# A depthwise convolution of 31 taps, wholly as multiply-adds on VectorE

## The chip, the cores and the metric

The kernel runs on one core of one Trainium2 chip. The metric is the device time of one execution in microseconds (us). A core has five engines that run side by side, each in its own order: TensorE (PE; its weight loads are shown as PEld), VectorE (DVE), ScalarE (ACT), GpSimd (POOL) and SyncE (SP), which issues DMAs.

## The reference

A two-layer hybrid backbone over 256 latent and 256 context tokens, width 1024. Layer 0 runs attention (8 heads, 2 key/value heads) beside a convolution module of 512 channels; both share one input projection `w_in` and one output projection `w_o`. A SwiGLU follows, then a Mamba-2 layer and a mixture of 8 experts. The change lies in `conformer_conv`:

```python
def depthwise_conv(x, w, b):
    width = w.shape[0]                                   # 31
    y = lax.conv_general_dilated(x, w[:, None, :].astype(x.dtype), window_strides=(1,),
                                 padding=[(width // 2, width // 2)],
                                 dimension_numbers=('NWC', 'WIO', 'NWC'),
                                 feature_group_count=x.shape[-1])
    return y + b

def conformer_conv(u, dw_w, dw_b, ln_g, ln_b):
    a, g = jnp.split(u, 2, axis=-1)
    h = depthwise_conv(a * jax.nn.sigmoid(g), dw_w, dw_b)
    return jax.nn.silu(layer_norm(h, ln_g, ln_b))

def even_mixer(...):
    ...
    a_lat = latent_attention(q, k, v, kc, vc)
    b_lat = conformer_conv(u, dw_w, dw_b, ln_g, ln_b)
    y = jnp.concatenate([a_lat, b_lat], axis=-1) @ w_o
    ...
```

The context tokens go through the same functions with the same weights.

## The kernel before

Tokens lie along the free dimension (512: two streams `s` of 256), channels on the 128 partitions, so the convolution's 512 channels are four chunks of 128x512. A product in full precision is three matmuls (`mm3`, lines 243 to 245): each factor is split into a high part that TensorE reads exactly and a rest. For weights ScalarE casts the high part (L161) and VectorE subtracts (L164), 128x1024 at a time; for activations the same is done by L133 and L134.

`even_u` computes the two halves of the projection; at its end VectorE multiplies them into `pad` (L527), four chunks with 15 zeros on each side of a stream, and starts the generator `even_conv` in the background. `even_conv` takes the chunks in two pairs. Tap 0 is ScalarE's (L545). Taps 1 to 17 are multiply-adds on VectorE, `scalar_tensor_tensor` (L568): `acc = pad[shifted] * weight + acc`, one for each tap and chunk, 68 in all, 128x512 each. Taps 18 to 30 (`NPE = 13`) are products on TensorE: for each tap and chunk ScalarE multiplies the identity by the tap's weights into a diagonal matrix (`dg`, L559), GpSimd makes the diagonal of their rest (L560), and `mm3` accumulates into one PSUM bank (`c<-t,dg`): 52 taps, 156 matmuls. For these `pad` is split once a chunk (L133, L134), and at the end VectorE adds the bank to `acc` (L573), four times. The tap weights are split in `columns2` (L314, L315).

`even_ln` follows on the same generator, across the 512 channels, which are partitions: products with a matrix of ones sum the four chunks (L583, c = 0 to 3) to the mean (L585); the chunks are centred (L589), squared (L591) and summed again (L593); VectorE reduces (L597), GpSimd makes the factor (L428, L430), TensorE broadcasts it (L602). Then each chunk is multiplied (L607), goes through silu on ScalarE (L609), and is split (L133, L134) into the factors k = 4 to 7 of the output projection; k = 0 to 3 come from attention.

What is written first: `phase1` goes through a list of units (the key/value and q projections, the groups of adaLN matmuls, L347, whose weights come by DMA), and after each piece of weights `tick` lets each background generator run to its next `yield` (the convolution once, an attention generator twice). So the convolution's taps, the attention (q and k norms L635 to L661, scores L752, transposes of probabilities L784, products with V L775) and the projections are interleaved. After the list, `drain` finishes the generators, and the units of `w_o` follow (`g<-whl,t` in the trace). A scheduler then fixes each engine's order from dependences and its own clock; on the chip each engine runs its list strictly in that order.

Of the kernel before, what the change touches and what calls it, by code (L numbers as in the profile page):

```python
# [10 lines left out]
F32 = mybir.dt.float32  # L11
F32R = mybir.dt.float32r
# [3 lines left out]
ALU = mybir.AluOpType  # L16
# [3 lines left out]
P = 128  # L20
# [70 lines left out]
class Net:  # L91
# [210 lines left out]
    def columns2(self):  # L302
        A, cols, row = self.A, self.cols_fn, self.row_fn
        kc = self.ecp.tile([P, NCONST - C_LE], F32, name="kc")
        self.nc.sync.dma_start(kc, A["kc"][:, C_LE:NCONST])
        self.LE, self.GE, self.GT = (kc[:, c - C_LE:c - C_LE + P] for c in (C_LE, C_GE, C_GT))
        self.cosd, self.sind = (kc[:, c - C_LE:c - C_LE + P].rearrange("p (b d) -> p b d", b=2) for c in (C_COS, C_SIN))
        c2 = cols("c2", [row(A["ev_norm2"][0]), row(A["ev_dw_b"][0]), row(A["ev_ln_g"][0]), row(A["ev_ln_b"][0])], self.wp)
        self.n2e, self.dwb, self.lng, self.lnb = c2[:, 0:8], c2[:, 8:12], c2[:, 12:16], c2[:, 16:20]
        w = cols("dww", [A["ev_dw_w"][0].rearrange("t (c p) -> (t c) p", p=P)], self.wp)  # L310
        self.dww = w.rearrange("p (t c) -> p t c", c=4)
        wh = self.wp.tile([P, 124], F32R, name="dwh")
        wl = self.wp.tile([P, 124], F32, name="dwl")
        self.nc.scalar.copy(wh, w)  # L314
        self.nc.vector.tensor_sub(wl, w, wh.bitcast(F32))  # L315
        self.dwl = wl.rearrange("p (t c) -> p t c", c=4)

    def columns3(self):
        A, cols, row = self.A, self.cols_fn, self.row_fn
# [74 lines left out]
    def row(self, col):  # L394

        nc = self.nc
        pt = self.ps()
        nc.tensor.transpose(pt[:8, 0:P], col, self.ident)
        r = self.wk([8, P], "row", bufs=1)
        nc.scalar.copy(r, pt[:8, 0:P])  # L400
        d = self.drp.tile([8, P], F32, name=self.nm("drow"))
        nc.sync.dma_start(d, r)
        return d
# [86 lines left out]
    R_NORM = 1  # L490


    NPE = 13

    def even_u(self, h):

# [40 lines left out]
    def even_conv(self):  # L537

        nc = self.nc
        nd = 31 - self.NPE  # L540
        for c0 in (0, 2):
            acc, hl = [], []
            for c in (c0, c0 + 1):
                a = self.cacc[:, c].rearrange("p (s t) -> p s t", s=2)
                nc.scalar.activation(a, self.pad[:, c, :, 0:256], AF.Identity, scale=self.dww[:, 0, c:c + 1],  # L545
                                     bias=self.dwb[:, c:c + 1])
                acc.append(a)
                x = self.wk([P, 2, 2, 286], "t8", F32R)
                self.split(x[:, 0], x[:, 1], self.pad[:, c])
                hl.append(x)  # L550
            pe = [(j, t) for j in range(2) for t in range(nd, 31)]
            n = max(nd - 1, self.NPE)
            done = None
            for i in range(n):
                for j, t in pe[2 * i:2 * i + 2]:
                    if t == nd:
                        pc = self.ps("c")
                    d = [self.wk([P, P], f"dg{q}", F32R, bufs=4) for q in range(2)]
                    nc.scalar.mul(d[0], self.ident, self.dww[:, t, c0 + j:c0 + j + 1])  # L559
                    nc.gpsimd.tensor_scalar(d[1], self.ident, self.dwl[:, t, c0 + j:c0 + j + 1], None,  # L560
                                            op0=ALU.mult)
                    self.mm3(pc.rearrange("p (s t) -> p s t", s=2), d,
                             (hl[j][:, 0, :, t:t + 256], hl[j][:, 1, :, t:t + 256]), t == nd, t == 30)
                    if t == 30:
                        done = j, pc
                if i + 1 < nd:
                    for j in range(2):
                        nc.vector.scalar_tensor_tensor(acc[j], self.pad[:, c0 + j, :, i + 1:i + 257],  # L568
                                                       self.dww[:, i + 1, c0 + j:c0 + j + 1], acc[j],
                                                       op0=ALU.mult, op1=ALU.add)  # L570
                if done:
                    j, q = done
                    nc.vector.tensor_tensor(acc[j], acc[j], q.rearrange("p (s t) -> p s t", s=2), op=ALU.add)  # L573
                    done = None
                yield
        yield from self.even_ln()

# [1297 lines left out]
```

## Time and profile before

| | before |
|---|---|
| median of 3 runs | 1913.47 us (1911.69 to 1915.6) |
| profiled execution | 1911.85 us, span 1910.1 us, mean granted TensorE clock 0.961 |
| TensorE busy | 1778.9 us, 93% of the span (weight loads 58%) |
| VectorE busy | 703.5 us, 37% |
| ScalarE busy | 519.1 us, 27% |
| GpSimd busy | 174.1 us, 9% |

The span begins with the profiled execution's first instruction; rows give microseconds from there. Shares over the span mix stages with different limits: the expert stage, most of the span, is TensorE and DMA with VectorE almost idle, and the convolution lies between 88 and 200 us. TensorE takes a matmul of two 32-bit factors as two records, so a count in a row can be twice the program's. The record of an instruction may overlap the next one's: where the text speaks of spacing it is the time from one start to the next.

### The profile page before, as it was taken

How to read it: one execution, taken by the hardware profiler on the slowest of the kernel's cores; microseconds unless marked ns; L12 is line 12 of the kernel's file. 1: busy time of each engine (PE TensorE's matmuls, PEld its weight loads, DVE VectorE, ACT ScalarE, POOL GpSimd, SP SyncE). 2: the span in 40 equal slices, each digit the busy share in tenths (PEclk: the TensorE clock that was granted, in tenths of full speed). 3: DMA queues.
4: the chain of work that ended last, by engine and by line, in shares of the span. 5: the costliest groups of instructions: out<-in, count | busy, mean ns of one | idle time of the engine just before them, and what ended most of it. 6: DMA issues, size and time to landing. Idle time of an engine off the chain costs nothing. (4 is left out here: it accounts for less than half of the span.)

```text
span 1910.1 us, 33591 instructions
## 1 busy us (share of the span) xinstructions
PE 1778.9 (93%) x14384; PEld 1110.9 (58%) x14384; DVE 703.5 (37%) x1143; ACT 519.1 (27%) x969; POOL 174.1 (9%) x167
## 2 busy tenths in 40 slices
PE   6999998999999989989989999999999999899964
PEld 3675356788888868757667445445644463435411
DVE  3395546334334356798887110101110101002001
ACT  3434454231222335756874100100000000001000
POOL 0064000000000014133320000000000000000000
PEclk8999999999999999989899899999999999999976
DMA  8543765422323243323357899999999999999995
GB/s 319 178 157 120 250 184 189 135 96 89 109 89 98 81 142 103 122 84 115 101 197 279 320 399 418 416 418 416 418 416 417 417 417 412 414 419 413 417 413 230
DMA packets 131574, 497.87 MB, mean 261 GB/s; under 512 B 11312, under 2 KB 18392, under 8 KB 102744
## 3 DMA queue, kind: packets, MB, share of 16 engines
q1 hardware_dynamic: 126808, 487.25, 66.3%
q10 hardware_dynamic: 4608, 8.39, 1.3%
q8 instruction: 115, 1.88, 0.4%
q14 instruction: 43, 0.35, 0.1%
HBM read 494.45 MB, written 1.15 MB: 259 GB/s over the span
## 5 line engine op out<-in xcount | busy, mean ns | idle before, releaser
L1533 PE MATMUL h<-raw,xe 128*32 128x512 f32 (+1 forms) x2664 | 265.6, 551 | 15.8 <-DMA raw<-in_od_ex_w_dram 15.8
L244 PE MATMUL g<-t,whl 128*128 128x512 f32 (+1 forms) x608 | 237.4, 390 | 0.0
L243 PE MATMUL g<-t,whl 128*128 128x512 f32 (+1 forms) x608 | 234.8, 396 | 2.1 <-ACT opad L1057 1.9
L245 PE MATMUL g<-t,whl 128*128 128x512 f32 (+1 forms) x608 | 232.7, 390 | 0.8 <-POOL whl L164 0.8
L1533 PE MATMUL h<-t,xe 128*32 128x384 f32 (+1 forms) x2200 | 214.9, 543 | 7.7 <-DMA t<-in_od_ex_w_dram 7.7
L164 DVE TENSOR_TENSOR whl<-raw,whl 128x1024 fp32r<-128x1024 f32 x109 | 137.7, 1266 | 206.6 <-ACT whl L161 206.1
L161 ACT CAST whl<-raw 128x1024 fp32r<-128x1024 f32 x129 | 134.5, 1049 | 269.9 <-PE g L245 234.3
L1533 PEld LDWEIGHTS h<-raw,xe 128*32 128x32 f32 x2664 | 97.8, 111 | 175.2 <-issue 113.2
L1544 DVE TENSOR_TENSOR g<-g,h 128x512 f32<-128x512 f32 (+1 forms) x38 | 23.6, 621 | 425.9 <-PE h L1533 238.6
L244 PE MATMUL g<-whl,t 128*128 128x512 f32 (+1 forms) x432 | 168.0, 392 | 9.2 <-DVE whl L164 7.3
L245 PE MATMUL g<-whl,t 128*128 128x512 f32 (+1 forms) x432 | 164.4, 389 | 0.0
L243 PE MATMUL g<-whl,t 128*128 128x512 f32 (+1 forms) x432 | 160.5, 394 | 1.9 <-DVE t L641 1.8
L1533 PEld LDWEIGHTS h<-t,xe 128*32 128x32 f32 x2200 | 79.1, 110 | 136.1 <-issue 91.8
L1598 PE MATMUL y<-raw,hT 128*32 128x256 f32 x2512 | 144.7, 388 | 9.7 <-DMA raw<-in_od_ex_w_dram 9.7
L1541 ACT ACTIVATE g<-h 128x512 f32<-128x512 f32 (+1 forms) x38 | 20.7, 544 | 448.9 <-PE h L1533 448.9
L243 PEld LDWEIGHTS g<-t,whl 128*128 128x128 f32 x608 | 116.6, 192 | 29.3 <-ACT opad L1057 2.3
L244 PEld LDWEIGHTS g<-t,whl 128*128 128x128 f32 x608 | 116.3, 191 | 23.7 <-issue 1.0
L245 PEld LDWEIGHTS g<-t,whl 128*128 128x128 f32 x608 | 115.4, 190 | 24.2 <-POOL whl L164 1.0
L428 POOL TENSOR_SCALAR rsv<-sst 128x1 f32<-128x1 f32 (+1 forms) x15 | 4.7, 311 | 1295.0 <-DVE sst L421 1294.8
L1598 PEld LDWEIGHTS y<-raw,hT 128*32 128x32 f32 x2512 | 80.0, 112 | 72.4 <-DMA raw<-in_od_ex_w_dram 15.0
L1598 PE MATMUL y<-t,hT 128*32 128x256 f32 x1744 | 103.4, 395 | 10.7 <-DMA t<-in_od_ex_w_dram 10.7
L1612 DVE TENSOR_TENSOR ys<-y,g2r 128x512 f32<-128x512 f32 (+1 forms) x12 | 6.6, 577 | 260.6 <-PE y L1598 260.6
(349 smaller groups left out, 2091.1 us busy)
## 6 DMA issues: line engine op xcount, KB each, us to landing
raw<-in_od_ex_w_dram SPq DMA_DIRECT2D x138, 1024.0 KB, 18.0
t<-in_od_ex_w_dram SPq DMA_DIRECT2D x102, 1024.0 KB, 19.2
raw<-in_od_ex_w_dram SPq DMA_DIRECT2D x68, 768.0 KB, 15.0
t<-in_od_ex_w_dram SPq DMA_DIRECT2D x60, 768.0 KB, 15.8
raw<-in_ev_ff_w_dram SPq DMA_DIRECT2D x32, 1024.0 KB, 5.1
raw<-in_ev_ada_w_dram SPq DMA_DIRECT2D x24, 1024.0 KB, 6.7
raw<-in_od_ada_w_dram SPq DMA_DIRECT2D x24, 1024.0 KB, 5.2
raw<-in_od_w_in_dram SPq DMA_DIRECT2D x20, 1024.0 KB, 5.2
```

Source lines behind the costliest of these rows:

```text
L161: self.nc.scalar.copy(hv, v[:, k0:k0 + m])
L164: eng.tensor_tensor(lv, v[:, k0:k0 + m], hv.bitcast(F32), op=ALU.subtract)
L243: mm(out, l[0], r[0], start=start, stop=False)
L244: mm(out, l[0], r[1], start=False, stop=False)
L245: mm(out, l[1], r[0], start=False, stop=stop)
L428: nc.gpsimd.tensor_scalar(v[:, :m], ss, inv_n, EPS, op0=ALU.mult, op1=ALU.add)
L1533: nc.tensor.matmul(st[i][g][32 * p:32 * p + 32, :n], st["x"][:, k, 32 * g:32 * g + 32], wv[:, n * p:n * p + n], start=k == 0, stop=k == KD ...
L1541: nc.scalar.activation(st["g"][g], st[0][g][:, :n], AF.Silu)
L1544: nc.vector.tensor_mul(st["g"][g], st["g"][g], st[1][g][:, :n])
L1598: nc.tensor.matmul(st["y"][g // 2][32 * q:32 * q + 32, g % 2 * 256:g % 2 * 256 + 256], st["hT", s][:, c, g, 32 * p:32 * p + 32], wv[:, 256 ...
L1612: nc.vector.tensor_tensor(ys[:, g:g + m], st["y"][g // 2][:, :256 * m].rearrange("p (g n) -> p g n", g=m), self.g2.unsqueeze(1).to_broadca ...
```

## The change

`even_conv` computes all of the taps 1 to 30 as multiply-adds on VectorE, 120 where there were 68. Each turn (from one `yield` to the next) holds one tap of both chunks of a pair, so a pair has 30 turns where it had 17. The diagonals, their 156 matmuls, the split of `pad`, the four additions from PSUM and the split of the tap weights are gone. `even_ln` and all else are as before; lines behind the change carry lower numbers (L568 is L543 now, L583 is L554, L602 is L573, L347 is L342, L752 is L723, L784 is L755, L660 is L631, L661 is L632, L637 is L608, L641 is L612, L653 is L624, L687 and L707 and others fall likewise).

```diff
--- before.py
+++ after.py
@@ -309,11 +309,6 @@
         self.n2e, self.dwb, self.lng, self.lnb = c2[:, 0:8], c2[:, 8:12], c2[:, 12:16], c2[:, 16:20]
         w = cols("dww", [A["ev_dw_w"][0].rearrange("t (c p) -> (t c) p", p=P)], self.wp)
         self.dww = w.rearrange("p (t c) -> p t c", c=4)
-        wh = self.wp.tile([P, 124], F32R, name="dwh")
-        wl = self.wp.tile([P, 124], F32, name="dwl")
-        self.nc.scalar.copy(wh, w)
-        self.nc.vector.tensor_sub(wl, w, wh.bitcast(F32))
-        self.dwl = wl.rearrange("p (t c) -> p t c", c=4)
 
     def columns3(self):
         A, cols, row = self.A, self.cols_fn, self.row_fn
@@ -490,7 +485,6 @@
     R_NORM = 1
 
 
-    NPE = 13
 
     def even_u(self, h):
 
@@ -537,41 +531,18 @@
     def even_conv(self):
 
         nc = self.nc
-        nd = 31 - self.NPE
         for c0 in (0, 2):
-            acc, hl = [], []
+            acc = []
             for c in (c0, c0 + 1):
                 a = self.cacc[:, c].rearrange("p (s t) -> p s t", s=2)
                 nc.scalar.activation(a, self.pad[:, c, :, 0:256], AF.Identity, scale=self.dww[:, 0, c:c + 1],
                                      bias=self.dwb[:, c:c + 1])
                 acc.append(a)
-                x = self.wk([P, 2, 2, 286], "t8", F32R)
-                self.split(x[:, 0], x[:, 1], self.pad[:, c])
-                hl.append(x)
-            pe = [(j, t) for j in range(2) for t in range(nd, 31)]
-            n = max(nd - 1, self.NPE)
-            done = None
-            for i in range(n):
-                for j, t in pe[2 * i:2 * i + 2]:
-                    if t == nd:
-                        pc = self.ps("c")
-                    d = [self.wk([P, P], f"dg{q}", F32R, bufs=4) for q in range(2)]
-                    nc.scalar.mul(d[0], self.ident, self.dww[:, t, c0 + j:c0 + j + 1])
-                    nc.gpsimd.tensor_scalar(d[1], self.ident, self.dwl[:, t, c0 + j:c0 + j + 1], None,
-                                            op0=ALU.mult)
-                    self.mm3(pc.rearrange("p (s t) -> p s t", s=2), d,
-                             (hl[j][:, 0, :, t:t + 256], hl[j][:, 1, :, t:t + 256]), t == nd, t == 30)
-                    if t == 30:
-                        done = j, pc
-                if i + 1 < nd:
-                    for j in range(2):
-                        nc.vector.scalar_tensor_tensor(acc[j], self.pad[:, c0 + j, :, i + 1:i + 257],
-                                                       self.dww[:, i + 1, c0 + j:c0 + j + 1], acc[j],
-                                                       op0=ALU.mult, op1=ALU.add)
-                if done:
-                    j, q = done
-                    nc.vector.tensor_tensor(acc[j], acc[j], q.rearrange("p (s t) -> p s t", s=2), op=ALU.add)
-                    done = None
+            for t in range(1, 31):
+                for j in range(2):
+                    nc.vector.scalar_tensor_tensor(acc[j], self.pad[:, c0 + j, :, t:t + 256],
+                                                   self.dww[:, t, c0 + j:c0 + j + 1], acc[j],
+                                                   op0=ALU.mult, op1=ALU.add)
                 yield
         yield from self.even_ln()
 
```

VectorE, around the split of the last q weights (`L164 whl`), in the second pair of chunks; `t_55` is the convolution's accumulator, `kn`, `gs`, `gc` and `ss` belong to the norm and rotation of k and q. Before:

```order
L568 SCALAR_TENSOR_TENSOR t_55_261<-pad_262,dww,t_55_261 128x512
L661 TENSOR_TENSOR kn_1107<-t_209_1116,t_210_1118 128x128
L568 SCALAR_TENSOR_TENSOR t_55_261<-pad_262,dww,t_55_261 128x512
L659 TENSOR_TENSOR t_219_1166<-t_218_1164,gs_477 128x64 x2
L568 SCALAR_TENSOR_TENSOR t_55_261<-pad_262,dww,t_55_261 128x512
L660 TENSOR_TENSOR t_218_1164<-t_218_1164,gc_476 128x128
L164 TENSOR_TENSOR whl_995<-raw_913,whl_995 128x1024
L661 TENSOR_TENSOR kn_1155<-t_218_1164,t_219_1166 128x128
L637 TENSOR_REDUCE ss_1204<-t_222_1202 128x8
L641 TENSOR_TENSOR t_226_1210<-g_1000,rs_1208 128x512
```

And with the change:

```order
L543 SCALAR_TENSOR_TENSOR t_55_261<-pad_262,dww,t_55_261 128x512 x4
L631 TENSOR_TENSOR t_162_968<-t_162_968,gc_472 128x128
L164 TENSOR_TENSOR whl_828<-raw_760,whl_828 128x1024
L543 SCALAR_TENSOR_TENSOR t_55_261<-pad_262,dww,t_55_261 128x512 x4
L632 TENSOR_TENSOR kn_959<-t_162_968,t_163_970 128x128
L543 SCALAR_TENSOR_TENSOR t_55_261<-pad_262,dww,t_55_261 128x512 x4
L608 TENSOR_REDUCE ss_1008<-t_166_1006 128x8
L543 SCALAR_TENSOR_TENSOR t_55_261<-pad_262,dww,t_55_261 128x512 x6
L612 TENSOR_TENSOR t_170_1014<-g_833,rs_1012 128x512
L543 SCALAR_TENSOR_TENSOR t_55_261<-pad_262,dww,t_55_261 128x512 x4
L624 TENSOR_TENSOR t_134_832<-t_170_1014,qkg_469 128x2x4x64
```

Single multiply-adds stood between two steps of the norms; now there are up to six. The split stands behind 69 of the 120 multiply-adds; in the program before it was behind 54 of 68.

TensorE, around the products with ones that sum the chunks (`c<-t_55,ones`), between the attention's scores (`g<-kT,t`), transposes (`t<-ka,pe`) and an adaLN group (`g<-raw,cs`). Before:

```order
L784 MATMUL t_1515<-ka,pe_1380 128x128
L784 MATMUL t_1515<-ka,pe_1397 128x128
L784 MATMUL t_1515<-ka,pe_1437 128x128
L583 MATMUL c_2119<-t_55_261,ones 128x512 x3
L784 MATMUL t_1508<-ka,pe_1454 128x128
L784 MATMUL t_1515<-ka,pe_1454 128x128
L347 MATMUL g_1578<-raw_1410,cs 32x512 x4
L347 MATMUL g_1578<-raw_1467,cs 32x512 x4
L752 MATMUL g_1599<-kT_841,t_181_998 128x256
```

And with the change:

```order
L723 MATMUL g_1161<-kT_702,t_133_831 128x256
L723 MATMUL g_1186<-kT_702,t_133_831 128x256
L554 MATMUL c_1850<-t_55_261,ones 128x512
L723 MATMUL g_1187<-kT_702,t_133_831 128x256
L723 MATMUL g_1203<-kT_702,t_133_831 128x256
L678 MATMUL t_1093<-ka,t_134_832 128x128 x4
L723 MATMUL g_1204<-kT_702,t_133_831 128x256
L554 MATMUL c_1850<-t_55_261,ones 128x512 x3
L342 MATMUL g_1222<-raw_1099,cs 32x512 x4
```

The products of chunks 1 to 3 stand earlier among the attention's work, ahead of the transposes of probabilities. Between them and the first product of `w_o` TensorE's list now holds 8 scores of 256 columns where it held 4, 72 adaLN matmuls where it held 64, 96 transposes of probabilities where it held 90, 4 transposes of q where it held none; the product of chunk 3, which stood there alone, is gone from there.

TensorE, behind the broadcast of the layer norm's factor (`c<-ka,rs`); `t_272` before and `t_205` with the change are the high part of k = 4 of the output projection, the first chunk behind silu, and `t_271`, `t_273`, `t_204`, `t_206` are factors that come from attention. Before:

```order
L243 MATMUL g_2287<-whl_2256,t_271_1372 128x512
L244 MATMUL g_2287<-whl_2256,t_271_1372 128x512
L602 MATMUL c_2222<-ka,rs_2199 128x128 x4
L245 MATMUL g_2287<-whl_2256,t_273_1374 128x512
L243 MATMUL g_2285<-whl_2259,t_271_1372 128x512
...
L245 MATMUL g_2288<-whl_2259,t_273_1374 128x512
L398 MATMUL t_2418<-ka,ac_114 8x128
L243 MATMUL g_2285<-whl_2264,t_272_1373 128x512
```

And with the change:

```order
L244 MATMUL g_1952<-whl_1923,t_204_1139 128x512
L245 MATMUL g_1952<-whl_1923,t_206_1141 128x512
L393 MATMUL t_2082<-ka,ac_114 8x128
L393 MATMUL t_2089<-ka,ac_114 8x128
L573 MATMUL c_1892<-ka,rs_1890 128x128 x4
L342 MATMUL c_2257<-raw_2127,cs 32x512 x4
L342 MATMUL c_2257<-raw_2129,cs 32x512 x4
L243 MATMUL g_1949<-whl_1928,t_205_1140 128x512
L244 MATMUL g_1949<-whl_1928,t_205_1140 128x512
```

Thirty products of the output projection that need no silu stood between the broadcast and the first that does; now an adaLN group of 8 matmuls (`c<-raw,cs`) stands there alone, and those products are ahead of the broadcast. That group stood in the stage behind `w_o` before.

## Rows read from the trace of the kernel before

**Rows 1.** Busy time in two stretches (us; in brackets the instructions); granted clock; DMA share
```profile
core 0: us, PE busy (x) PEld busy (x) DVE busy (x) ACT busy (x) POOL busy (x), PEclk, DMA share, GB/s
89.00:198.00 109.00, 103.81 (x535) 70.92 (x533) 87.51 (x164) 46.19 (x112) 55.38 (x64) 0.97 0.42 147
198.00:270.00 72.00, 68.15 (x334) 26.36 (x330) 34.71 (x84) 32.35 (x76) 0.00 (x0) 1.00 0.68 213
```

**Rows 2.** Costliest groups: shapes, count | busy us, mean ns | idle ahead, what ended it
```profile
L568 DVE SCALAR_TENSOR_TENSOR t<-pad,dww,t 128x512 f32<-128x512 f32 x68 | 49.6, 765 | 0.0
L243 PE MATMUL c<-t,dg 128*128 128x512 f32 x52 | 21.5, 414 | 1.1 <-DVE t L573 1.1
L560 POOL TENSOR_SCALAR dg<-ka,dwl 128x128 fp32r<-128x128 f32 x52 | 44.3, 865 | 104.8 <-DVE dwl L315 53.9 <-PE c L245 50.5
```

**Rows 3.** TensorE in order of time: start, duration us, line, tiles, count
```profile
98.53 0.39 PE L243 MATMUL c<-t,dg 128*128 128x512 f32 x1
...
100.63 0.40 PE L243 MATMUL c<-t,dg 128*128 128x512 f32 x1
```

**Rows 4.** ScalarE in order of time, one cast of the key and value weights
```profile
102.40 2.00 ACT L161 CAST whl<-raw 128x1024 fp32r<-128x1024 f32 x2 [0.64 <-DMA raw<-in_ev_w_in_dram]
```

**Rows 5.** VectorE in order of time, first half of the convolution
```profile
88.86 2.06 DVE L527 TENSOR_TENSOR pad<-t,t 128x512 f32<-128x512 f32 x3 [11.24 <-ACT t L526]
...
97.37 7.64 DVE L568 SCALAR_TENSOR_TENSOR t<-pad,dww,t 128x512 f32<-128x512 f32 x10
104.93 0.68 DVE L355 TENSOR_TENSOR ar<-ar,t 128x512 f32<-128x512 f32 x1
105.53 1.21 DVE L164 TENSOR_TENSOR whl<-raw,whl 128x1024 fp32r<-128x1024 f32 x1
...
111.84 2.72 DVE L568 SCALAR_TENSOR_TENSOR t<-pad,dww,t 128x512 f32<-128x512 f32 x4
114.49 0.67 DVE L573 TENSOR_TENSOR t<-t,c 128x512 f32<-128x512 f32 x1
...
119.54 0.27 DVE L637 TENSOR_REDUCE ss<-t 128x2 f32<-128x128 f32 x1
```

**Rows 6.** VectorE in order of time, a wait and the last multiply-add
```profile
150.27 0.69 DVE L637 TENSOR_REDUCE ss<-t 128x8 f32<-128x512 f32 x1 [3.76 <-ACT t L635]
...
197.03 0.75 DVE L568 SCALAR_TENSOR_TENSOR t<-pad,dww,t 128x512 f32<-128x512 f32 x1
197.69 0.61 DVE L764 TENSOR_SCALAR pe<-pe,rc 128x256 f32<-128x256 f32 x2
```

**Rows 7.** TensorE in order of time, around the matmuls with ones
```profile
191.81 1.13 PE L752 MATMUL g<-kT,t 64*128 64x256 f32 x6
...
193.25 2.88 PE L583 MATMUL c<-t,ones 128*128 128x512 f32 x6
...
195.97 0.38 PE L784 MATMUL t<-ka,pe 128*128 128x128 f32 x2
196.28 1.92 PE L347 MATMUL g<-raw,cs 128*32 128x512 f32 x16
...
200.97 1.12 PE L583 MATMUL c<-t,ones 128*128 128x512 f32 x2
```

**Rows 8.** TensorE in order of time, the broadcast of the layer norm's factor
```profile
276.93 1.05 PE L602 MATMUL c<-ka,rs 128*128 128x128 f32 x8
```

**Rows 9.** ScalarE in order of time, the layer norm's last step
```profile
279.70 0.26 ACT L400 COPY row<-t 8x128 f32<-8x128 f32 x1 [4.05 <-DMA drow<-row]
279.98 1.28 ACT L609 ACT_TABLE_LOAD   x1
...
282.70 0.60 ACT L133 CAST t<-t 128x512 fp32r<-128x512 f32 x1
```

**Rows 10.** Busy time and granted clock behind a wait of TensorE, columns as in group 1
```profile
154.00:156.00 2.00, 2.00 (x12) 0.53 (x8) 0.43 (x1) 0.00 (x0) 0.00 (x0) 0.50 0.00 0
```

**Rows 11.** TensorE in order of time, the group of matmuls behind that wait
```profile
153.80 3.62 PE L347 MATMUL g<-raw,cs 128*32 128x512 f32 x16 [2.04 <-issue]
```

## The prediction, made before the changed kernel was run

> **What bounds the kernel now.** First the windows, by engine, for the stretch of the convolution and the one behind it [rows 1]. From 89 to 198 us TensorE is busy for 103.81 of 109 us at a granted clock of 0.97, VectorE for 87.51. From 198 to 270, to the start of the output projection, TensorE is busy for 68.15 of 72 us, VectorE for 34.71. So TensorE is nearly full in both, VectorE has 21.5 us free in the first and 37 in the second, and the change takes from the fuller engine and gives to the one that has room, but only in the first stretch can it give: there the convolution lives.
>
> Next the groups of the convolution [rows 2]: 68 multiply-adds on VectorE, 49.6 us of records, 765 ns each; 52 diagonals' rests on GpSimd, 865 ns each; and the first of the three matmuls of each tap, 52 of them. In TensorE's order of time nine diagonal matmuls stand 0.233 us apart [rows 3]: from 98.53 to 100.63. Then VectorE's timeline [rows 5, 6]: the first multiply into `pad` starts at 88.86, the last multiply-add starts at 197.03 and ends by 197.78. Last, TensorE around the products with ones [rows 7]: three of the four end at 195.97, ahead of the last multiply-add, and TensorE goes on at once with other work; the fourth comes at 200.97. So before, the end of the convolution holds nobody up. The question is whether the longer chain on VectorE still ends in time.
>
> **What is taken from TensorE.** 156 matmuls by 0.233 us are 36.4 us of TensorE. About 45 of them ran before 105 us, while the key and value weights were still awaited (ScalarE's cast of them waited for their DMA until 102.40 [rows 4]), where they cost nothing; the other 111 are 25.9 us. That is the most the change can give, and it gives it only if nothing else ends last. GpSimd's and ScalarE's diagonals go as well; neither engine was the bound.
>
> **What a multiply-add costs.** Two rows bear on it. Ten in a row from 97.37 to 104.93 start 0.756 us apart while GpSimd is making diagonals; four in a row from 111.84 to 114.49 start 0.6625 us apart while it is not [rows 5]. With the change GpSimd makes none, so I take 0.6625. Bounds: a plain two-input operation of the same size takes 0.60 from start to start (104.93 to 105.53 [rows 5]), and the full record of one is 0.75 (197.03 [rows 6]; the average, 0.765, includes the stretches beside GpSimd).
>
> **When the convolution ends now.** The new order of VectorE holds, from the first multiply into `pad` to the last multiply-add, 120 multiply-adds, 6 weight splits, 21 operations that read 512 columns and 38 small ones. 120 x 0.6625 = 79.5 us. The splits at 1.21 [rows 5] are 7.3. The 21 at 0.60 are 12.6. The small ones lie between 0.17 and 0.34; the reduction at 119.54 has 0.27 [rows 5], two of 256 columns take 0.61 together [rows 6]; at 0.25 they make 9.5. Sum 108.9 us: from 88.86 to 197.8. The splits at their full record leave some tenths for waits in this sum. That there are almost none I take from the order: the norm's reduction before waited 3.76 us for ScalarE's squares at 150.27 [rows 6]; now four multiply-adds, 2.65 us, stand ahead of it and four to six ahead of the steps behind it, so the 21.5 idle us are filled. By totals it comes out alike: 87.51 busy, plus 52 x 0.6625 = 34.5, less four splits of `pad` and four additions of some 0.67 each, 5.4, makes 116.6 us of records for 109 us of time, 7.6 too many; what has no room is other VectorE work, which the new order puts behind the last tap, where 37 us are free. I take the last multiply-add to end at 198.0.
>
> **What waits for it.** In TensorE's new list the products with ones of chunks 1 to 3 stand ahead of most of the attention. Chunk 2 is ready 0.66 us ahead of chunk 3, so one product lies on the path, 0.91 us at full clock (a third of 195.97 less 193.25 [rows 7]); TensorE has been starved for the last stretch and has to come back from the lower clock. What that costs the rows show: behind an idle stretch of 2.04 us the granted clock was 0.50, and the same adaLN group that takes 1.92 at 196.28 took 3.62 [rows 7, 10, 11]. I charge one product at twice its time, 1.8 (bounds 0.9 and 0.9 + 1.7 = 2.6 and a little more where the clock stays down longer). So TensorE passes this place at 199.8; before, at 195.97: **+3.85**.
>
> Behind this place TensorE now has more to do than before, since work that it could do early now stands behind the wait: four scores of 256 columns (0.38 each, from six records in 1.13 us [rows 7]) are 1.5, one adaLN group 1.9 [rows 7], ten transposes at 0.155 (two in 0.31, 195.97 to 196.28 [rows 7]) 1.55; less the fourth product with ones, 0.91. Sum **+4.0** (0 at the least, if the 3.85 us in which TensorE was idle from 198 to 270 [rows 1] swallow it).
>
> **The layer norm's tail.** Before, the broadcast ended at 277.98 [rows 8] and the first silu chunk was split at 283.30 [rows 9], 5.3 us later, and thirty products of the output projection, 30 x 0.23 = 6.9 us, ran meanwhile: hidden. Now an adaLN group of 1.9 us stands there alone, so 5.3 - 1.9 = 3.4 us are open. In these 5.3 ScalarE came to the silu's table load late, at 279.98, behind a copy that waited 4.05 us for a DMA [rows 9]; without it the chunk's multiply, some 0.65, sets the start, 1.3 us sooner, and 2.1 are open. I take the middle, **+2.8** (0 if the chain beats TensorE there, 5.3 if that group's weights come late). The adaLN group itself is only moved: it is missing from the stage behind, so it cancels.
>
> Sum: 3.85 + 4.0 + 2.8 = +10.65 us, all on TensorE's path, which stays nearly full to the end of the layer, so later stages carry it one for one. 1911.85 + 10.65 = 1922.5 for a profiled execution; the median lies 1.6 us above the profiled one, so **1924 us**.
>
> **Rivals.** About 0.2%, 3.8 us, is what a measurement of this kernel tells from no change: "same" is 1909.6 to 1917.3.
>
> *Faster: TensorE's relief counts.* If multiply-adds without GpSimd beside them run closer than the four in rows 5 let see, the convolution ends in time and up to 25.9 us come back: 1913.5 - 25.9 = 1888 at the far end. For a gain that can be measured the sum has to fall by 14.5 us, 0.12 us from each of 120: a spacing under 0.54. No operation of 512 columns has less than 0.60. For it speaks only that so much is to be had. Chance 0.13.
>
> *Same: a tap costs what a plain operation does.* With 0.60 from start to start 120 x 0.0625 = 7.5 us go: +3.2, 1917; the same comes of an idle TensorE behind 198 that swallows the 4.0 together with a short tail. Chance 0.18.
>
> *Slower by twice as much: a tap costs its whole record.* If each multiply-add waits until the one ahead has written its last element, 120 end to end stand a record apart: 120 x (0.75 - 0.6625) = 10.5 us more, 1934.5. The trace speaks against it, since four stand in 2.65 us where four records are 3.0, and ten beside GpSimd in 7.56. The Trainium skill ("VectorE: DVE Perf Modes", section "The DRAIN you can't avoid") has it so: the next VectorE operation doesn't start until the pipe of the one before has emptied. By that rule the time would be this rival's; the trace does not agree. The same time comes if VectorE keeps half of its 21.5 idle us, because TensorE, starved and at the lower clock, delivers q late. Chance 0.14.
>
> *The forecast*, slower by 4 to 17 us, 1917 to 1930, has the rest, 0.55. So faster 0.13, same 0.18, slower 0.55 + 0.14 = 0.69. The range, which leaves out the far end of the gain and the far end of the lower clock, is 1909 to 1936; the forecast's own is 1917 to 1930.
>
> **What would show it.** In the changed profile VectorE should be busy from 89 to 198 without a gap over a microsecond or two, multiply-adds 0.66 us apart, the last ending near 198; TensorE should show idle time in that stretch that ends with a release by VectorE's last multiply-add at the product with ones, with a granted clock below 0.97; that product should end near 200 and the output projection begin some 8 us later than at 270; and behind the broadcast TensorE should wait 2 to 3 us for the split behind silu. If the multiply-adds stand under 0.6 us apart, or if the products with ones end ahead of 196, the sum is wrong from its first term; if VectorE waits within the stretch for q or k, the end lies late and the time nearer to 1934.

## The result and the profile after

The changed kernel takes 1924.69 us in the median of 5 runs (1924.27 to 1928.49), the kernel before 1913.47 (5 runs); the ratio is 1.0072, 95% interval 1.0058 to 1.0085. The profiled execution is the longest of the five, 1928.49 us with a span of 1926.7 us and a mean granted clock of 0.948; a second profile of the same kernel (below, the run "again") has 1923.55 and 1921.8. Where the two differ, both are given.

The windows of the changed kernel, columns as in [rows 1]:

```profile
core 0: us, PE busy (x) PEld busy (x) DVE busy (x) ACT busy (x) POOL busy (x), PEclk, DMA share, GB/s
89.00:198.00 109.00, 72.14 (x325) 46.94 (x324) 107.21 (x186) 21.04 (x42) 17.03 (x16) 0.75 0.37 127
198.00:270.00 72.00, 70.21 (x331) 25.00 (x329) 36.16 (x98) 31.96 (x83) 0.00 (x0) 0.97 0.62 211
190.00:200.00 10.00, 9.93 (x16) 4.22 (x17) 10.00 (x26) 2.63 (x9) 0.00 (x0) 0.50 0.00 0
```

This is [rows 1] turned over: VectorE went from 87.51 to 107.21 of 109 us, TensorE from 103.81 to 72.14, and TensorE's clock from 0.97 to 0.75. In the last 10 us of the convolution TensorE has the lower level, 1.2 GHz, throughout.

VectorE in order of time; `L543` are the multiply-adds:

```profile
110.95 5.39 DVE L543 SCALAR_TENSOR_TENSOR t<-pad,dww,t 128x512 f32<-128x512 f32 x8
...
153.93 2.73 DVE L543 SCALAR_TENSOR_TENSOR t<-pad,dww,t 128x512 f32<-128x512 f32 x4
156.58 0.67 DVE L608 TENSOR_REDUCE ss<-t 128x8 f32<-128x512 f32 x1
157.18 4.05 DVE L543 SCALAR_TENSOR_TENSOR t<-pad,dww,t 128x512 f32<-128x512 f32 x6
...
188.62 1.40 DVE L543 SCALAR_TENSOR_TENSOR t<-pad,dww,t 128x512 f32<-128x512 f32 x2
...
197.71 0.74 DVE L543 SCALAR_TENSOR_TENSOR t<-pad,dww,t 128x512 f32<-128x512 f32 x1
```

Eight multiply-adds take 5.39 us, seven steps of 0.66 and a last record; the last of all starts at 197.71 and ends at 198.45. The reduction of the norm, for which VectorE waited 3.76 us in [rows 6], has no wait in brackets now; from the first multiply into `pad` to the last multiply-add VectorE waits three times, 1.8 us in all.

TensorE around the products with ones (`L554`; before: [rows 7]):

```profile
190.07 2.07 PE L554 MATMUL c<-t,ones 128*128 128x512 f32 x2 [5.94 <-DVE t L543]
192.07 2.34 PE L723 MATMUL g<-kT,t 64*128 64x256 f32 x4
194.34 1.11 PE L678 MATMUL t<-ka,t 128*128 128x128 f32 x4
195.39 1.22 PE L723 MATMUL g<-kT,t 64*128 64x256 f32 x2
196.54 5.49 PE L554 MATMUL c<-t,ones 128*128 128x512 f32 x6
201.95 1.92 PE L342 MATMUL g<-raw,cs 128*32 128x512 f32 x16
```

The first, that of chunk 0, waits 5.94 us for a multiply-add, the one that ends at 190.02 (188.62 and 1.40); seven more follow it on VectorE. From there to 201.95 no row of TensorE has a wait: everything runs at half speed, three products in 5.4 us, 1.8 each, where they took 0.91 before. The product of chunk 3 starts at about 200.1 (196.54 and two products of 1.8), 1.7 us behind the end of the last multiply-add, so it did not wait for it. TensorE leaves this place at 201.95; before, at 195.97. In the second profile the last two rows read

```profile
197.02 5.47 PE L554 MATMUL c<-t,ones 128*128 128x512 f32 x6
202.42 1.92 PE L342 MATMUL g<-raw,cs 128*32 128x512 f32 x16
```

Next the output projection. Its first product and the first that needs silu, before:

```profile
270.50 0.94 PE L243 MATMUL g<-whl,t 128*128 128x512 f32 x3
...
284.89 0.48 PE L243 MATMUL g<-whl,t 128*128 128x512 f32 x1
```

And after, with the sums of squares (`L564`) and the broadcast (`L573`):

```profile
276.40 0.96 PE L243 MATMUL g<-whl,t 128*128 128x512 f32 x3 [0.17 <-ACT whl L161]
...
285.90 3.63 PE L564 MATMUL c<-ones,t 128*128 128x1 f32 x32
...
291.02 0.63 PE L243 MATMUL g<-whl,t 128*128 128x512 f32 x1
291.45 0.63 PE L244 MATMUL g<-whl,t 128*128 128x512 f32 x1
...
295.88 1.06 PE L573 MATMUL c<-ka,rs 128*128 128x128 f32 x8
```

```profile
299.56 2.38 PE L342 MATMUL c<-raw,cs 128*32 128x512 f32 x16 [2.62 <-issue]
301.87 0.80 PE L243 MATMUL g<-whl,t 128*128 128x512 f32 x1
```

The four multiplies behind the broadcast on VectorE, and ScalarE's last steps of the layer norm (before: [rows 9]):

```profile
296.97 2.48 DVE L578 TENSOR_TENSOR t<-t,c 128x512 f32<-128x512 f32 x4 [3.41 <-PE c L573]
```

```profile
298.37 1.52 ACT L580 ACTIVATE t<-t,c 128x512 f32<-128x512 f32 x2
299.80 0.60 ACT L133 CAST t<-t 128x512 fp32r<-128x512 f32 x1
```

The sums of squares now stand inside the projection, behind them products run 0.43 us apart instead of 0.23 (291.02 to 291.45) at the lower level, as the window of these 3 us shows,

```profile
291.00:294.00 3.00, 3.00 (x8) 2.31 (x7) 1.23 (x1) 1.04 (x1) 0.11 (x1) 0.50 0.00 0
```

and behind the broadcast TensorE idles for 2.62 us. From 270.50 to 284.89 it was 14.4 us before; from 276.40 to 301.87 it is 25.5, with the same 48 products of the projection, but the sums of squares and the adaLN group stand in it now.

### The profile page after: what moved, and what is told of

Its sections match the earlier page's. It is cut to its first block, busy times and chain, and to the rows that moved or that the text cites. A ratio compares the mean times of both kernels' runs of the same rounds, so it can differ in the third digit from the quotient of the medians.

```text
span 1926.7 us, 33167 instructions
## 1 busy us (share of the span) xinstructions
PE 1763.3 (92%) x14228; PEld 1091.2 (57%) x14228; DVE 728.4 (38%) x1186; ACT 499.0 (26%) x912; POOL 135.4 (7%) x115
## 5 line engine op out<-in xcount | busy, mean ns | idle before, releaser
L1504 PE MATMUL h<-raw,xe 128*32 128x512 f32 (+1 forms) x2664 | 266.1, 552 | 14.4 <-DMA raw<-in_od_ex_w_dram 14.4
L164 DVE TENSOR_TENSOR whl<-raw,whl 128x1024 fp32r<-128x1024 f32 x109 | 137.8, 1267 | 204.0 <-ACT whl L161 200.3
L1515 DVE TENSOR_TENSOR g<-g,h 128x512 f32<-128x512 f32 (+1 forms) x38 | 23.6, 621 | 426.0 <-PE h L1504 239.7
L243 PE MATMUL g<-whl,t 128*128 128x512 f32 (+1 forms) x432 | 164.4, 406 | 16.9 <-DVE t L612 8.1
L244 PE MATMUL g<-whl,t 128*128 128x512 f32 (+1 forms) x432 | 172.3, 401 | 5.5 <-DVE whl L164 3.8
L245 PE MATMUL g<-whl,t 128*128 128x512 f32 (+1 forms) x432 | 167.1, 394 | 0.0
L1569 PEld LDWEIGHTS y<-raw,hT 128*32 128x32 f32 x2512 | 79.7, 111 | 74.2 <-DMA raw<-in_od_ex_w_dram 16.6
L243 PEld LDWEIGHTS g<-whl,t 128*128 128x128 f32 x432 | 84.0, 196 | 42.5 <-issue 10.9
```

What stands on the lines that cost most here:

```text
L164: eng.tensor_tensor(lv, v[:, k0:k0 + m], hv.bitcast(F32), op=ALU.subtract)
L243: mm(out, l[0], r[0], start=start, stop=False)
L244: mm(out, l[0], r[1], start=False, stop=False)
L245: mm(out, l[1], r[0], start=False, stop=stop)
L1504: nc.tensor.matmul(st[i][g][32 * p:32 * p + 32, :n], st["x"][:, k, 32 * g:32 * g + 32], wv[:, n * p:n * p + n], start=k == 0, stop=k == KD ...
L1515: nc.vector.tensor_mul(st["g"][g], st["g"][g], st[1][g][:, :n])
```

## The experiments

My theory: what costs is VectorE's list up to the last multiply-add; TensorE, behind it, is starved (it waits without work), comes back at half clock and then waits for the layer norm's last steps (its tail). Rivals: the starved clock by itself; the layer norm's tail by itself; the amount of VectorE's work, wherever it stands. Ratios are to the kernel before, with 95% intervals.

**The changed kernel again** (no edit).

> The changed kernel itself, unaltered, since its profiled execution (1928.5 us) lies 3.8 us above its median: a second profile and times beside the next three kernels. Every theory: a median of 1924 to 1925, some 11 us above the kernel before. In the trace the last multiply-add ends at 198.4 again and the three products with ones at 201 to 202 under a granted clock of 0.5; if the shift by the end of the layer is nearer 12 than 16.6 us, the difference lies in waits behind the convolution that vary from run to run.

Measured 1.0071 (1.0054 to 1.0088). The products with ones end at 202.42. That is 0.5 us later than in the first profile; at the start of the odd layer (the Mamba-2 layer, below) it is 2.7 us earlier, 751.0 against 753.7, so what makes the first profile long arises behind the convolution. About half of it stands in the layer norm's tail: in the second profile the adaLN group behind the 2.62 idle us takes 1.92 instead of 2.38 us, and the products behind it start 0.23 us apart at once, where in the first profile four steps keep 0.43.

**Thirteen taps left out.** The edit:

```diff
-            for t in range(1, 31):
+            for t in range(1, 18):
```

> Leaves out the taps 18 to 30 altogether: 68 multiply-adds on VectorE as before, no products on TensorE. My theory (the 52 added multiply-adds hold the end, the relief of TensorE is real but covered): VectorE is done early, the relief of some 26 us counts, less a layer-norm tail of about 3: 1889 to 1895 us. Rival A (taking TensorE's work away starves it and lowers its clock, whatever VectorE does): little or nothing gained, 1908 to 1920. Rival B (the loss is made only behind the convolution, in the layer norm's tail): about 1913 + 3.

This kernel leaves taps 18 to 30 out of the computation, so its tokens go to other experts and its total (4240 us, with 1201 MB read from HBM where the changed kernel reads 494) says nothing. It is read where the odd layer's convolution begins, ahead of the experts, by the first of 24 copies into that layer's input tile; the two times at the end of a row are the first and the last start. The kernel before, the changed one (second profile), and the one without the taps:

```profile
L1057 ACT COPY opad<-g x24: 355/576/606, 735.5 to 936.5; 128x512 f32<-128x512 f32 x20, 128x256 f32<-128x256 f32 x4
```
```profile
L1028 ACT COPY opad<-g x24: 354/576/598, 751.0 to 951.5; 128x512 f32<-128x512 f32 x20, 128x256 f32<-128x256 f32 x4
```
```profile
L1028 ACT COPY opad<-g x24: 353/570/597, 728.4 to 927.7; 128x512 f32<-128x512 f32 x20, 128x256 f32<-128x256 f32 x4
```

The 52 multiply-adds are worth 751.0 - 728.4 = 22.6 us there, 0.43 each; the 156 matmuls and all that belonged to them 735.5 - 728.4 = 7.1. Each kernel gives one profile here, and the two of the changed kernel lie 2.7 us apart at this place, so both numbers are good to a few us. I had expected some 20: with 68 multiply-adds VectorE is still busy for 83.75 of the 109 us and TensorE idles for 23.6 of them at a mean clock of 0.80. Its longest waits end with steps of the q and k norms (4.0 and 3.4 us) and with casts of the weights (4.0); so most of the relief turned into waits. The difference of the two, 15.5, is the shift of the changed kernel at this place.

**Three taps more**, into a tile that nobody reads:

```diff
+            x = self.wk([P, 512], "scr", bufs=1).rearrange("p (s t) -> p s t", s=2)
+            for t in (1, 2, 3):
+                for j in range(2):
+                    nc.vector.scalar_tensor_tensor(x, self.pad[:, c0 + j, :, t:t + 256],
+                                                   self.dww[:, t, c0 + j:c0 + j + 1], acc[j],
+                                                   op0=ALU.mult, op1=ALU.add)
+                yield
```

> The changed kernel with three more multiply-adds for each chunk into a tile that nobody reads (12 in all, 8.0 us of VectorE). My theory (VectorE is full to the last multiply-add and TensorE waits for it): 4 to 8 us slower than the changed kernel, less than in proportion since the list lets five more scores ahead: ratio 1.009 to 1.011. Rival (VectorE's length is not what counts): no change, 1.007.

Measured 1.0114 (1.0090 to 1.0138), 0.43% or 8.2 us above the changed kernel, against 12 x 0.6625 = 8.0. The two intervals together leave some 3 to 14 us, and the last multiply-add starts at 211.9, 13.7 us later than in the second profile of the changed kernel, since the list puts other steps ahead of it too. So more VectorE work ahead of the products costs time; that a multiply-add costs just its spacing is not shown.

**TensorE kept busy.** One matmul a turn whose result nobody reads:

```diff
             for t in range(1, 31):
+                nc.tensor.matmul(self.ps("c")[:, 0:256], self.ones, self.pad[:, c0, 0, t:t + 256], start=True, stop=True)
```

> The changed kernel with one matmul of 256 columns in each turn whose result nobody reads (60 of them, some 27 us of TensorE), to keep TensorE from standing idle in the convolution. My theory: the end of VectorE's chain stays at 198.4, the products with ones then run at full clock and end near 199.5 instead of 202, so 2 to 3 us come back: 1921.5 to 1923. Rival (the whole loss is the half clock): back to 1913 to 1916. Rival (TensorE still has no room in this stretch): later than 1924.7 by up to 27 us.

Measured 1.0102 (1.0085 to 1.0118), a median of 1930.4 us: not the gain that I expected, but the third rival's number, later than 1924.7. The windows of the second profile of the changed kernel and of this one, to 180 us and behind:

```profile
89.00:180.00 91.00, 61.69 (x306) 42.22 (x304) 88.91 (x148) 17.16 (x33) 14.79 (x14) 0.80 0.44 152
180.00:200.00 20.00, 12.31 (x22) 5.60 (x23) 20.00 (x44) 4.80 (x14) 2.27 (x2) 0.50 0.00 0
```

```profile
89.00:180.00 91.00, 88.75 (x431) 55.32 (x430) 86.91 (x145) 16.79 (x31) 14.39 (x14) 1.00 0.43 152
180.00:200.00 20.00, 8.82 (x22) 3.72 (x20) 20.00 (x41) 5.00 (x12) 2.27 (x2) 0.61 0.00 1
```

Up to 180 us the clock is at its full level and TensorE busy for 88.75 of 91 us, and VectorE's chain ends no earlier (its last multiply-add starts at 201.4, not 198.2). So a full clock up to there does not by itself bring the end forward. But the added matmuls fill the room that TensorE had, and what the low clock alone costs up to there this run does not show. Behind 180 the added matmuls are used up and TensorE is starved as before, at 0.61; what the products with ones would take at full clock stays open too, and with it the rival of the starved clock.

**Two turns after each piece**, so that the layer norm comes earlier:

```diff
-    R_CONV = 1
+    R_CONV = 2
```

> The changed kernel with two turns of the convolution after each piece instead of one, so the layer norm behind it is written ahead of the attention's later steps; VectorE's list to the last multiply-add and TensorE's to the products with ones stay as they are. My theory: only the exposed tail of the layer norm goes, 3 to 5 us (2.6 idle and the half clock behind it): 1919.5 to 1922. Rival (the tail costs nothing, all is lost at the products with ones): 1924 to 1925. Rival (the layer norm's small steps, put earlier, delay the attention): above 1926.

Measured 1.0075 (1.0053 to 1.0098): no change. The tail is closed, as meant; silu, four instructions, starts at 263.5 instead of 298.7:

```profile
L580 ACT ACTIVATE t<-t,c x4: 800/807/817, 263.5 to 266.2; 128x512 f32<-128x512 f32 x4
```

but the attention, whose turns the layer norm took, ends later (the last product with V starts at 296.0, in the second profile of the changed kernel at 284.0), and other waits stand behind it:

```profile
PE g L342 <- DMA raw<-in_od_ada_w_dram: 2.6, 1, 2.6
```

An open tail of 2.6 us is therefore not what the change loses: closing it moved the wait.

**The weight splits on GpSimd.** In the stretch of the convolution alone:

```diff
             self.later(self.even_conv(), self.R_CONV)
+            self.lo_mix = (0,)
...
+        self.lo_mix = (1,)
         wo, ff = self.even_out(), self.ffn(h2, self.f1[n[3]:12 - self.N_N2])
```

> The changed kernel with the six weight splits of the convolution's stretch on GpSimd (2.9 us each there) instead of VectorE (1.14 each): VectorE is 6.8 us shorter, less some 2 us because its multiply-adds run at 0.756 beside GpSimd. My theory (the end of VectorE's chain sets when TensorE goes on): the last multiply-add ends near 194 instead of 198.5, and the time falls by 3 to 5 us against the changed kernel: ratio to before 1.0035 to 1.0055. Rival (the loss lies in the lower clock and the layer norm's tail alone): no change, 1.007.

Measured 1.0095 (1.0079 to 1.0111), 0.24% above the changed kernel, which is about as much as the two intervals can tell apart, and the last multiply-add starts at 199.8, later and not 4.5 us earlier. VectorE's timeline, GpSimd's beside it, and the multiply-adds by duration (least, median, most, in ns):

```profile
107.62 22.48 DVE L544 SCALAR_TENSOR_TENSOR t<-pad,dww,t 128x512 f32<-128x512 f32 x19
```

```profile
105.20 9.47 POOL L164 TENSOR_TENSOR whl<-raw,whl 128x1024 fp32r<-128x1024 f32 x3 [93.38 <-ACT whl L161]
117.94 2.85 POOL L164 TENSOR_TENSOR whl<-raw,whl 128x1024 fp32r<-128x1024 f32 x1 [3.27 <-ACT whl L161]
123.69 2.55 POOL L164 TENSOR_TENSOR whl<-raw,whl 128x1024 fp32r<-128x1024 f32 x1 [2.90 <-ACT whl L161]
```

```profile
L544 DVE SCALAR_TENSOR_TENSOR t<-pad,dww,t x120: 730/739/2887, 91.1 to 199.8; 128x512 f32<-128x512 f32 x120
```

Nineteen multiply-adds take 22.48 us, where nineteen at 0.66 take 12.6. Beside each of the six splits one multiply-add lasts until about 0.5 us behind the split's end: the longest has 2887 ns, a split 2.85 us, and the rest keep 0.74. So the edit did not shorten VectorE and doesn't test the theory.

**Between the two kernels: 9, 6 and 4 taps on TensorE.** The kernel before with another constant:

```diff
-    NPE = 13
+    NPE = 9    # 6, 4
```

> The kernel before with 9 taps of a chunk on TensorE instead of 13: 84 multiply-adds on VectorE (16 more, 10.6 us), 108 diagonal matmuls (48 fewer, 11.2 us). My theory (VectorE's added work costs nothing until its idle 21.5 us in the convolution are used up, and TensorE's relief is worth a quarter of its size, as the run without the 13 taps shows by the end of the layer): 2 to 4 us faster than the kernel before, ratio 0.998 to 0.999. Rival (each added multiply-add costs its share of the 12 us at once): 16/52 of it, 3.7 us slower, 1.002. Rival (TensorE's relief counts in full): 11 us faster, 0.994.

> The same with 6 taps on TensorE: 96 multiply-adds (28 more, 18.6 us), 72 diagonal matmuls (84 fewer, 19.6 us). My theory: VectorE's room is about used up, the relief still a quarter: 0 to 5 us faster, ratio 0.9975 to 1.000. Rival (in proportion): 28/52 of 12 us, 6.5 us slower, 1.0034.

> The same with 4 taps on TensorE: 104 multiply-adds (36 more, 23.9 us), 48 diagonal matmuls (108 fewer, 25.2 us). My theory: VectorE is over its room by 2.4 us and the splits of the input are still there; but in this kernel's list the products with ones stand behind most of the attention, so TensorE is not held up: between 3 us faster and 4 us slower, 0.9985 to 1.002. Rival (in proportion): 36/52 of 12 us, 8.3 us slower, 1.0043.

Measured 1.0024 (1.0006 to 1.0041), 0.9990 (0.9978 to 1.0003) and 1.0059 (1.0041 to 1.0076). Only the second came as I expected; the first and the third agree with the rival in proportion (1.002 and 1.0043). With 28 more multiply-adds there is no loss that can be told, with 16 there is a small one, with 36 most of the whole (0.59% of 0.71%): the number of multiply-adds alone does not give the time, and that rests on the run with 6 taps, where the rival needed 1.0034. With 4 taps the attention is on time (its last product with V starts at 274.6, before at 274.4), but the list has put the taps far back:

```profile
L568 DVE SCALAR_TENSOR_TENSOR t<-pad,dww,t x104: 731/743/857, 90.4 to 244.6; 128x512 f32<-128x512 f32 x104
```

The last starts at 244.6. Two of TensorE's waits from 89 to 400 us that the run with 6 taps does not have (total, times, longest) are for the attention's probabilities and for the layer norm's factor:

```profile
PE t L784 <- DVE pe L764: 4.5, 2, 4.3
PE c L602 <- POOL rs L430: 2.8, 1, 2.8
```

But with 6 taps, where nothing is lost, the last multiply-add starts later still:

```profile
L568 DVE SCALAR_TENSOR_TENSOR t<-pad,dww,t x96: 730/743/856, 91.7 to 249.7; 128x512 f32<-128x512 f32 x96
```

So a late end of VectorE's chain does not by itself cost time, and why 4 taps lose where 6 don't stays open.

**The same multiply-adds, placed later.** Tap 0 goes through the small ring `t2`, so that the second pair can't start before the attention frees a tile of it; no instruction is added:

```diff
-    R_CONV = 1
+    R_CONV = 2    # defer_r2; 1.5 in defer_r1_5
...
-                nc.scalar.activation(a, self.pad[:, c, :, 0:256], AF.Identity, scale=self.dww[:, 0, c:c + 1],
+                x = self.wk([P, 512], "t2").rearrange("p (s t) -> p s t", s=2)
+                nc.scalar.activation(x, self.pad[:, c, :, 0:256], AF.Identity, scale=self.dww[:, 0, c:c + 1],
                                      bias=self.dwb[:, c:c + 1])
-                acc.append(a)
+                acc.append((a, x))
             for t in range(1, 31):
                 for j in range(2):
-                    nc.vector.scalar_tensor_tensor(acc[j], self.pad[:, c0 + j, :, t:t + 256],
-                                                   self.dww[:, t, c0 + j:c0 + j + 1], acc[j],
+                    nc.vector.scalar_tensor_tensor(acc[j][0], self.pad[:, c0 + j, :, t:t + 256],
+                                                   self.dww[:, t, c0 + j:c0 + j + 1], acc[j][t == 1],
                                                    op0=ALU.mult, op1=ALU.add)
```

> The changed kernel with the same 120 multiply-adds, but tap 0 of each chunk goes through a tile of the small ring that the attention uses too, so that the second pair of chunks can't start before the attention has freed one; and two turns after each piece. VectorE's list then has 112 other operations ahead of the last multiply-add instead of 66: the attention comes first and the taps run on into the stretch behind 198 us, where VectorE had 37 us free. My theory (what costs is that the attention and the products with ones stand behind a full VectorE, not the amount of VectorE's work): most of the loss goes, ratio to the kernel before 0.998 to 1.002. Rival (the added 34 us of VectorE cost their 12 us wherever they stand): 1.006 to 1.008. Rival (a convolution that ends later leaves the layer norm's tail open): slower than the changed kernel.

> The same with three turns after two pieces: 139 other operations ahead of the last multiply-add, the products with ones behind 28 scores and 64 transposes, and the broadcast of the layer norm again just ahead of the products that need it. My theory: TensorE is held up even less at the products with ones, but the layer norm's tail of some 3 to 5 us is open: 1.000 to 1.003. Rival (amount): 1.006 to 1.008. Rival (the tail is all): above 1.007.

Measured 1.0027 (1.0013 to 1.0040) and 1.0023 (1.0009 to 1.0037). Two thirds of the loss are gone with the same 120 multiply-adds. It is the ring that does it: with two turns after each piece and without the ring it was 1.0075. What the ring changes is the order of the chunks. The program writes the second pair behind the first, but the scheduler of the changed kernel takes all four chunks in turn from the third multiply-add on, so that chunk 0, the first to be done, gets its last as the 113th of 120. (VectorE's order above is said to lie in the second pair of chunks; with the change its multiply-adds are of both pairs.) With the ring the first sixty belong to the first pair, and its two products with ones run 44 us sooner than chunk 0's did at 190.07; the row of the second, with two records for each product:

```profile
146.37 1.98 PE L555 MATMUL c<-t,ones 128*128 128x512 f32 x4 [1.71 <-DVE t L544]
```

The last multiply-add starts at 216.4 and 231.1 in the two, later than the 198 of the changed kernel. The windows of the second:

```profile
89.00:198.00 109.00, 86.68 (x436) 52.39 (x436) 99.38 (x196) 30.79 (x72) 17.05 (x16) 0.84 0.49 167
198.00:270.00 72.00, 63.90 (x273) 23.56 (x271) 47.95 (x96) 29.98 (x66) 0.00 (x0) 0.95 0.62 191
```

TensorE does 86.68 us of its work ahead of 198 instead of 72, VectorE 47.95 behind it instead of 36.16. The amount of VectorE's work is the same; it is used where there was room. The rival "amount" falls, and so does the end of the last multiply-add as the measure of the loss; the last third, the 0.2% by which both stay slower than the kernel before, has no experiment of its own.

**Six taps on TensorE and three turns after two pieces** (`NPE = 6`, `R_CONV = 1.5`):

> The kernel before with 6 taps on TensorE and three turns of the convolution after two pieces, so that the layer norm is written ahead of part of the attention. My theory (in the run with 6 taps an open tail of the layer norm of 2.6 us and waits around it remain): 2 to 4 us faster than that run, ratio 0.997 to 0.998. Rival (nothing left to win there): 0.999.

Measured 1.0027 (1.0014 to 1.0039), slower than with one turn, not faster. As with two turns after each piece, the attention ends later: its last product with V starts at 285.7, with 6 taps alone at 271.2. No version beat the kernel before by more than can be told.

## Why the prediction came out right

**What a multiply-add costs and when the convolution ends: right.** 0.66 us each, and the end at 198.45 (198.0 was predicted; in the second profile the last starts 0.5 us later). The rivals for a tap at a plain operation's price or at its whole record needed 0.60 or 0.75; the rows show neither. That no operation of 512 columns has less than 0.60, as the prediction has it, holds for those with two tensors: multiplies of the probabilities by one factor a row (`pe<-pe,rc`, 128x512) have records of 0.48 to 0.49 us in the kernel before. The rule of the Trainium skill ("VectorE: DVE Perf Modes", "The DRAIN you can't avoid") that was weighed there, read so that a record ends with the empty pipe, does not hold for these rows: eight in a row keep 0.66 with records of 0.74. The same section of the Trainium skill lets an operation that is not held back start earlier, and the rows, 0.08 us ahead of the record's end, agree with that.

**TensorE's relief: right that it doesn't count,** and more so than I wrote: not only covered, but worth some 7 us where the bound of 25.9 stood, even with no more multiply-adds than before. (Of the diagonal matmuls 38 start before 105 us, not 45, so the bound should have been 27.5.) The rival "faster" could not have had its 25.9 us even if the added multiply-adds had cost nothing.

**The wait at the products with ones: the place right, the mechanism only in part, the size too small.** +3.85 was predicted, +5.98 (+6.45 in the second profile) measured. I had TensorE wait for the last multiply-add, with one product at half clock behind it, and took the first pair of chunks to be done early. The rows show another path: TensorE waits for the last multiply-add of chunk 0, to 190.07, and then runs for 11.9 us without a wait, four products with ones and the scores and transposes between them, all at half clock. The last multiply-add, at 198.45, held nothing up, and the sign that I gave, a wait that ends with it, is not in the rows; with one product at full clock behind it, 0.91, this place would have been passed at 199.4 (an estimate from these rows), so TensorE's own queue at half clock ends last, by some 2.6 us.

**More work behind: right.** +4.0 predicted. From the products with ones to the projection's start it is 74.45 us after and 74.53 before, but the sums of squares, 3.5 us, have moved out of it, so 3.4 were added net; TensorE's idle time from 198 to 270 fell from 3.85 to 1.79 us, so part of the added work went into it. For that reason the projection begins 5.9 us later, not some 8 as the prediction's last part has it.

**The layer norm's tail: the idle time right (2.62 for 2.8), its reason not as put.** I had let the adaLN group run during the chain. It starts at 299.56, 0.1 us after the last of VectorE's four multiplies ends (296.97 + 2.48 = 299.45), and writes a tile of the same PSUM tag, which has one bank; so by its place it waited for that bank and ran behind the chain, not beside it. That is read from the rows and was not tried. The chain itself was shorter than the 5.3 us of before, 3.5 from the broadcast's end (296.94) to the first split (300.40), so with the group beside it only some 1.6 us would have been open (an estimate from these rows): that 2.62 and 2.8 agree is chance. What I had missed is the half clock behind the sums of squares, seven steps of 0.43 instead of 0.23, 1.4 us, and in the first profile about as much again behind the 2.62 idle us.

**The sum.** +10.65 was predicted; the medians give 11.2, the ratio 13.8 (11.1 to 16.3), the two profiled executions 16.6 and 11.7. At the start of the odd layer the shift is 18.2 (753.7 in the first profile) and 15.5, so up to there the sum was 5 to 8 us too small, most of it half clock: 2.1 to 2.6 at the products with ones, some 1.5 to 3 in the output projection. At the end the shift is 16.6 and 11.7. So the shift was not carried one for one, as I had it: 2 to 4 us come back on the way, against the one profile of before, and whether that one had a chance wait there is open. That the median lies 0.7 us beside the predicted 1924 is therefore in part luck: two errors of opposite sign.

## What to carry to other kernels

Ask not how busy an engine is on average but whether its list still has room up to the operation for which the other engine waits: here VectorE had 21.5 us and got 29 net. Work that is taken from the fuller engine is worth what then ends last (some 7 of 36.4 us here), and when the emptied engine waits it also loses its clock (0.97 to 0.75 here). When moving work to another engine look at the order in which the scheduler really puts it there: the same 120 instructions, one pair of chunks after the other and the second one later, cost a third.

## What the runs showed of the hardware

Beside each of six two-input operations on GpSimd (the split, 128x1024, 2.85 us) one multiply-add on VectorE lasts up to 2887 ns where one takes 740, and ends just behind it, while beside the diagonals of the kernel before (one tensor and a scalar a partition) multiply-adds start 0.756 us apart instead of 0.6625. Moving 6.8 us of VectorE's work to GpSimd so lengthened VectorE's chain, by 1.6 to 2.1 us. And matmuls with one column, 32 of them in 3.5 us, count as busy in the rows, yet the granted clock fell to its lower level some 1.5 us behind them, with products of 512 columns running in between, in both profiles; what made it fall no run isolates.
